# A two-block transformer kernel on one core: the first FFN opens with eight gate/up pairs instead of four

## The chip, the cores and the metric

The kernel runs on one NeuronCore of one Trainium2 chip. The metric is the device time of one execution in microseconds (us), from the first to the last instruction with what lies around them. A core has five engines that run their own instruction streams in order: TensorE (PE, matrix products into PSUM), VectorE (DVE), ScalarE (ACT), GpSimd (POOL) and SyncE (SP), which here issues almost all loads from device memory. PSUM, the memory that PE accumulates into, has eight banks of 512 float32 columns per partition.

## The reference

Two blocks work on one sequence of 256 tokens with 1024 features. The part that matters here is the very beginning: an RMS norm, a modulation whose scale and shift come from products of a small condition vector `c` with a large matrix `ada_w`, and a SwiGLU feed-forward network (FFN).

```
def rms_norm(x, g):
    xf = x.astype(jnp.float32)
    y = xf * lax.rsqrt(jnp.mean(xf * xf, axis=-1, keepdims=True) + EPS)
    return (y * g.astype(jnp.float32)).astype(x.dtype)

def swiglu(h, w_in, w_out):
    gu = h @ w_in
    g, u = jnp.split(gu, 2, axis=-1)
    return (jax.nn.silu(g) * u) @ w_out
...
        mods = jnp.split(c_silu @ ada_w[layer] + ada_b[layer], N_MOD, axis=-1)
        sh, sc, g = mods[0], mods[1], mods[2]
        h = modulate(rms_norm(x, norm_g[layer, 0]), sh, sc)
        x = x + MACARON_WEIGHT * (1.0 + g)[:, None, :] * swiglu(h, ffn_w_in[layer, 0], ffn_w_out[layer, 0])
```

There are four such FFNs (two layers, two each), a pooling mixer, an attention, and then a second block with a state-space branch and another attention. The hidden width of an FFN is 2816, which is 22 blocks of 128.

## The kernel before

Activations lie transposed: 128 features on the partitions, 256 tokens along the free axis, eight such feature blocks (`KB`). All numbers are float32. To multiply them exactly enough, every weight and every activation is split into a high part `hi` (rounded by ScalarE, `whi`, `hhi`, `shi`) and the rest `lo` (subtracted on VectorE, `wlo`, `hlo`, `slo`), and each product of blocks is three matmuls: `hi·hi`, `lo·hi`, `hi·lo` (`mm3`).

**Weights.** `Stream` loads weights as tiles of 128 x 1024 float32 (512 KB, eight blocks of 128 x 128) in the fixed order of use, into five raw buffers `wraw`. `split` rounds a tile on ScalarE (line 225, `whi`) and subtracts on VectorE (line 216, `wlo`), into five buffers each; the raw buffer is then free. One tile feeds 8 x 3 = 24 matmuls of 256 columns. The first FFN uses 66 tiles: 44 for the gate and up matrices, 22 for the output matrix. This text numbers them 0 to 65.

**Modulation.** Scale, shift and gate columns are products of the condition with rows of `ada_w`: one load of 512 KB into one of three buffers `graw`, one VectorE instruction over 128 x 1024 (line 377, called a product below). The first FFN's own scale and shift need 16 products, two for each feature block; 45 more, needed later, are spread over the tiles of the first FFN by `plan` and `tick`, so many per tile (`ffn_plan` gives the weights: none for the first tiles, 1.0 for the other gate/up tiles, 1.2 for the output tiles down to the last five).

**Opening of the first FFN.** There, the norm and the modulation of the eight feature blocks come one after the other, so the FFN goes by feature block first: for each `k`, `feed(k)` makes block `k` of the activation (`hraw` and `hlo` on VectorE, `hhi` on ScalarE) and splits one weight tile, and PE adds that block's contribution to four gate/up pairs, which are eight accumulators, one in each PSUM bank. After the eighth `k` the four pairs are finished by `act` (silu on ScalarE, a multiply `sf` on VectorE, and the split into `shi` and `slo`), and the other 18 pairs follow one at a time, two tiles each. In each `feed(k)` the products for the next feature blocks are placed on VectorE between the other work.

**Order.** Each engine executes in the order in which the program issued to it, and so does SP's queue of loads: a load that waits for its buffer holds up the loads behind it. Nothing is reordered at run time.

Of the kernel before, what the change touches and what calls it, by code (L numbers as in the profile page):

```python
# [12 lines left out]
AF = mybir.ActivationFunctionType  # L13
# [3 lines left out]
D = 1024  # L17
T = 256
KB = 8
# [4 lines left out]
RAWB, HLB = 5, 5  # L24
LAG = 1
HEAD_LAG = 1
GRAW = 3
# [3 lines left out]
W_OUT = (1.2, 1.6, 1.5, 1.6)  # L31
# [3 lines left out]
SLOTS = 135  # L35
# [6 lines left out]
def lead(l, f):  # L42
    return 4 if (l, f) == (0, 0) else 2

# [150 lines left out]
def ffn_plan(skip, w):  # L195
    return [0.0] * skip + [1.0] * (44 - skip) + [w] * 17


class Stream:
# [37 lines left out]
    def next(self, hold=False, late=None):  # L237
        if not hold:
            self.split(self.nh + self.ahead, late)
        r = self.split_t.pop(self.nh)  # L240
        self.nh += 1
        if self.nh >= 6 and self.ahead < HLB - 1:
            self.ahead += 1
            self.depth = RAWB
        return r


class Kernel:
# [15 lines left out]

# [1 line left out]
    def pool(self, name, bufs=1, **kw):  # L266
# [79 lines left out]

# [1 line left out]
    def mm3(self, out, hi, lo, b, ah, al, first, last):  # L348
        mm = self.nc.tensor.matmul
        mm(out, hi[:, b], ah, start=first, stop=False)  # L350
        mm(out, lo[:, b], ah, start=False, stop=False)  # L351
        mm(out, hi[:, b], al, start=False, stop=last)  # L352
# [92 lines left out]

# [1 line left out]
    def st_begin(self, n):  # L447
# [100 lines left out]

# [1 line left out]
    def ffn(self, hh, hl, gate_fn, n0, gap, pre, feed=None):  # L550
        nc = self.nc
        with self.tc.tile_pool(name="ffn", bufs=1) as fp:
# [3 lines left out]
            def act(i, pg, pu):  # L556
# [7 lines left out]
                if i == FB - 1:  # L564
                    self.after()
            tags = ("AB", "DD", "AB", "CC")
            pp = [[self.ps(t) for t in tags[i]] for i in range(n0)]
            b = 0
            for k in range(KB):
                if feed:  # L570
                    feed(k)
                for i in range(n0):
                    for x in range(2):
                        if b % 8 == 0:
                            hi, lo = self.next()
                        self.mm3(pp[i][x][:, :T], hi, lo, b % 8, hh[:, k], hl[:, k], k == 0, k == 7)
                        b += 1
            for i in range(n0):
                self.defer(act, i, *pp[i], lag=1 + HEAD_LAG * i)
            for i in range(n0, FB):  # L580
                pg, pu = [self.ps(t) for t in tags[(i - n0 // 4) % 3]]
# [35 lines left out]

# [1 line left out]
    def pool_mixer(self, hh, hl, gate_fn, pre):  # L619
# [34 lines left out]

# [1 line left out]
    def qk_stats(self, p, nch, th, ssq):  # L656
# [207 lines left out]

# [1 line left out]
    def setup(self):  # L866
# [22 lines left out]
    def phase1(self):  # L889
# [12 lines left out]
        with ExitStack() as p1:  # L902
# [15 lines left out]
            self.adab = load("adab", [128, NADA])  # L918
            self.ws.dma(1)
            onesr = const.tile([1, 128], F32, name="onesr")  # L920
# [41 lines left out]
            for i in range(2):  # L962
                nc.tensor.matmul(pc[i], onesr, crow[:, i * 512:(i + 1) * 512], start=True, stop=True)
            for kb in range(4):
                self.st_add(self.X[:, kb], nc.vector)
            for i in range(2):
                nc.scalar.activation(self.cb[:, i * 512:(i + 1) * 512], pc[i], AF.Silu)
            self.st_add(self.X[:, 4], nc.vector)
            head_gemv(0, 0)
            for kb in range(5, 8):  # L970
                self.st_add(self.X[:, kb])
            nc.scalar.activation(self.cc[:, 0], self.cc[:, 0], AF.Silu)
            head_dma(1, 2)
            head_gemv(0, 1)
            self.st_half(D)
            head_dma(2, 3)
            rb = self.st_finish()
            head_gemv(1, 0)
            weights = [0, 0, 3, 4, 5, 6, 7, 8, 9, 10, 11]
            splits = [1, 2, 3, 4, 5, 6, 7, 8]  # L980
# [11 lines left out]
            def feed(k):  # L992
                self.ws.ahead = self.ws.depth = 0
                c = slice(k, k + 1)
                a = slice(2 * k + 1, 2 * k + 2)
                V.scalar_tensor_tensor(g0[:, 0, c], self.modc[:, a], hg[:, 0, c], hg[:, 1, c],
                                       op0=OP.mult, op1=OP.add)
                a = slice(2 * k, 2 * k + 1)
                V.tensor_add(g0[:, 1, c], self.modc[:, a], self.adab[:, a])
                hr = self.mod_a(rbs, g0, h0[0], k)  # L1000
                if k + 1 < KB:
                    head_gemv(k + 1, 1)
                self.mod_b(hr, g0, h0[0], h0[1], k)
                self.ws.split(splits[k])
                if k + 2 < KB:
                    head_gemv(k + 2, 0)
                elif k + 1 == KB:
                    self.ws.ahead = self.ws.depth = 2
                if k + 3 < KB:
                    head_dma(k + 3, weights[k + 3])  # L1010
                else:
                    self.ws.dma(weights[k + 3])

# [7 lines left out]
            for l in range(2):  # L1021
# [7 lines left out]
                if l == 0:  # L1029
                    self.plan(self.gemvs(16, 64), ffn_plan(8, W_OUT[0]), ssm[0], SLOTS)  # L1030
                else:
                    self.plan(self.gemvs(base + 16, AT_A), ffn_plan(3, W_OUT[2]), ssm[3], SLOTS)
# [33 lines left out]

# [1 line left out]
    def vround(self, out, x, w):  # L1068
# [287 lines left out]

# [1 line left out]
    def hilo(self, hi, lo, src, w=None):  # L1358
# [500 lines left out]
```

## Time and profile before

| | |
|---|---|
| time, median of 3 runs | 1341.07 us (1338.28 to 1343.94) |
| span of the profiled execution | 1336.8 us |
| PE busy, share of the span | 96% |
| VectorE busy | 76% |
| ScalarE busy | 50% |
| mean rate of loads and stores over the span | 248 GB/s |

The span reaches from the first to the last instruction of one execution that was profiled; the page gives no other time for that execution. The runs without a profile are on the median 4.3 us above it, for what lies around the span. Busy shares are averages over stages that differ; what the change meets is read from the first 225 us.

### The profile page before, as it was taken

To read this page: it belongs to the slowest core of one execution; us is meant where nothing else is said; L and a number is where in the kernel's file an instruction comes from. 1 tells how busy PE (TensorE), PEld (TensorE's weight loads), DVE (VectorE), ACT (ScalarE), POOL (GpSimd) and SP (SyncE) were. 2 spreads that over 40 slices of the span, in tenths; PEclk is the share of its full clock that TensorE was granted. 3 is DMA by queue.
4 is the path that set the end of the run, shared out by engine and by line. 5 is a ranking of instruction groups with operands and counts; after the bars stand their busy time and mean duration, and the time that the engine had idled before them with its cause. 6 is when DMAs were issued, how large, how long until landed. Compare 5 with 4: busy or idle time off the path is not lost.

```text
span 1336.8 us, 26399 instructions
## 1 busy us (share of the span) xinstructions
PE 1276.9 (96%) x10378; PEld 1212.9 (91%) x10378; DVE 1011.1 (76%) x1759; ACT 668.6 (50%) x1162; POOL 159.0 (12%) x273
## 2 busy tenths in 40 slices
PE   5899999999999999999998999999999899999998
PEld 4899998899999779999987989999988888989996
DVE  6898887788999689989967678777754476437774
ACT  3454434555444555544436555444465755337542
POOL 1000001100002100010111101000100791110000
PEclk9999999999999999999999999999998999999999
DMA  8999998497899577999975368878765533796752
GB/s 293 332 330 342 331 337 300 145 325 251 266 318 341 199 268 264 309 301 308 343 266 182 120 216 258 266 249 279 264 222 174 146 114 106 161 242 204 271 186 79
DMA packets 122287, 331.21 MB, mean 248 GB/s; under 512 B 27633, under 2 KB 42865, under 8 KB 122098
## 3 DMA queue, kind: packets, MB, share of 16 engines
q1 hardware_dynamic: 122018, 328.73, 73.5%
q8 instruction: 81, 1.33, 0.4%
q0 software_dynamic: 144, 0.79, 0.2%
q14 instruction: 44, 0.36, 0.1%
HBM read 317.94 MB, written 10.49 MB: 246 GB/s over the span
## 4 chain that ended last, share of the span: by engine, by line
PE 55%; ACT 4%; DVE 3%; DMA 2%; issue 1%; POOL 1%; SPq 0%; DVEq 0%; ACTq 0%; POOLq 0%
PE psA L350 5%; PE psA L352 4%; PE psB L350 4%; PE psB L351 4%; PE psB L352 4%; PE psA L351 4%; PE psD L350 3%; PE psD L352 3%; PE psD L351 3%; PE psC L350 2%; PE psC L352 2%; PE psC L351 2%; PE psA L356 1%; PE psA L357 1%; PE psA L358 1%
## 5 line engine op out<-in xcount | busy, mean ns | idle before, releaser
L216 DVE TENSOR_TENSOR wlo<-wraw,whi 128x1024 fp32r<-128x1024 f32 x391 | 478.5, 1230 | 45.3 <-ACT whi L225 44.9
L225 ACT CAST whi<-wraw 128x1024 fp32r<-128x1024 f32 x391 | 403.1, 1047 | 115.9 <-ACT whi L225 40.1
L377 DVE SCALAR_TENSOR_TENSOR junk<-graw,cb 128x1024 bf16<-128x1024 f32 x166 | 204.5, 1232 | 27.7 <-DMA graw<-in_ada 23.8
L350 PE MATMUL psD<-hhi,whi 128*128 128x256 f32 x560 | 161.6, 289 | 0.0
L352 PE MATMUL psD<-hlo,whi 128*128 128x256 f32 x560 | 160.5, 287 | 0.0
L351 PE MATMUL psD<-hhi,wlo 128*128 128x256 f32 x560 | 160.4, 286 | 0.0
L350 PE MATMUL psA<-hhi,whi 128*128 128x256 f32 x480 | 139.2, 290 | 4.9 <-ACT whi L225 3.4
L351 PE MATMUL psA<-hhi,wlo 128*128 128x256 f32 x480 | 137.7, 287 | 6.0 <-DVE wlo L216 6.0
L350 PE MATMUL psB<-hhi,whi 128*128 128x256 f32 x488 | 139.3, 285 | 0.0
L351 PE MATMUL psB<-hhi,wlo 128*128 128x256 f32 x488 | 138.9, 285 | 0.0
L352 PE MATMUL psB<-hlo,whi 128*128 128x256 f32 x488 | 138.8, 284 | 0.0
L352 PE MATMUL psA<-hlo,whi 128*128 128x256 f32 x480 | 137.1, 286 | 0.0
L350 PEld LDWEIGHTS psD<-hhi,whi 128*128 128x128 f32 x560 | 109.3, 195 | 2.0 <-issue 1.4
L352 PEld LDWEIGHTS psD<-hlo,whi 128*128 128x128 f32 x560 | 109.3, 195 | 0.0
L351 PEld LDWEIGHTS psD<-hhi,wlo 128*128 128x128 f32 x560 | 109.3, 195 | 0.0
L350 PEld LDWEIGHTS psA<-hhi,whi 128*128 128x128 f32 x480 | 93.0, 194 | 8.5 <-ACT whi L225 4.7
L351 PEld LDWEIGHTS psA<-hhi,wlo 128*128 128x128 f32 x480 | 93.2, 194 | 7.4 <-DVE wlo L216 7.3
L350 PE MATMUL psA<-shi,whi 128*128 128x256 f32 x352 | 99.3, 282 | 0.0
L352 PE MATMUL psA<-slo,whi 128*128 128x256 f32 x352 | 98.7, 280 | 0.0
L350 PE MATMUL psB<-shi,whi 128*128 128x256 f32 x352 | 98.6, 280 | 0.0
L352 PE MATMUL psB<-slo,whi 128*128 128x256 f32 x352 | 98.6, 280 | 0.0
L351 PE MATMUL psB<-shi,wlo 128*128 128x256 f32 x352 | 98.2, 279 | 0.0
(452 smaller groups left out, 3198.1 us busy)
## 6 DMA issues: line engine op xcount, KB each, us to landing
graw<-in_ada SPq DMA_DIRECT2D x184, 512.0 KB
wraw<-in_win SPq DMA_DIRECT2D x176, 512.0 KB
wraw<-in_w SPq DMA_DIRECT2D x93, 512.0 KB
wraw<-in_wout SPq DMA_DIRECT2D x88, 512.0 KB
wraw<-in_wkv SPq DMA_DIRECT2D x16, 512.0 KB
Hd<-ct SPq DMA_DIRECT2D x16, 256.0 KB
Gd<-gsb SPq DMA_DIRECT2D x16, 256.0 KB
wraw<-in_wq SPq DMA_DIRECT2D x8, 512.0 KB
```

The lines of the kernel that those rows point to most:

```text
L216: self.nc.vector.tensor_sub(lo, raw, hi.bitcast(F32))
L225: self.nc.scalar.copy(hi, raw)
L350: mm(out, hi[:, b], ah, start=first, stop=False)
L351: mm(out, lo[:, b], ah, start=False, stop=False)
L352: mm(out, hi[:, b], al, start=False, stop=last)
L356: mm(out, ah, whi, start=first, stop=False)
L357: mm(out, ah, wlo, start=False, stop=False)
L358: mm(out, al, whi, start=False, stop=last)
L377: self.nc.vector.scalar_tensor_tensor(junk, self.gemv_tile(j), 1.0, self.cb, op0=OP.mult, op1=OP.mult, accum_out=self.modc[:, j:j + 1])
```

## The change

- The first FFN opens with eight pairs instead of four. A pair's gate and up sums now share one PSUM bank, 256 columns each, so that eight pairs fill the eight banks. `feed(k)` splits two weight tiles instead of one, and PE does 48 matmuls for each `k` instead of 24.
- In `feed(k)` the order on VectorE changes: the first tile's `wlo` comes before `hlo`, and the two products stand behind the two `wlo`.
- `act` for the pairs of the opening is called as soon as a pair's last matmul is issued, instead of one per later tile.
- The first norm's sums of squares are all added on VectorE (two additions were on GpSimd), and the products around it move.
- Two weight tiles instead of one are loaded before the first products' loads, and two instead of one for each `k` after that.
- The 45 spread products are now spread over fewer tiles, since 16 tiles instead of 8 belong to the opening.

```diff
-HEAD_LAG = 1
+LEAD = 8
...
 def lead(l, f):
-    return 4 if (l, f) == (0, 0) else 2
+    return LEAD if (l, f) == (0, 0) else 2
...
-        if self.nh >= 6 and self.ahead < HLB - 1:
+        if self.nh >= 2 * LEAD - 2 and self.ahead < HLB - 1:
...
-            tags = ("AB", "DD", "AB", "CC")
-            pp = [[self.ps(t) for t in tags[i]] for i in range(n0)]
+            tags = ("AB", "DD", "AB")
             b = 0
-            for k in range(KB):
-                if feed:
+            if feed:
+                pp = [self.ps(t) for t in "ABDDABCC"[:n0]]
+                for k in range(KB):
                     feed(k)
+                    for i in range(n0):
+                        for x in range(2):
+                            if b % 8 == 0:
+                                hi, lo = self.next()
+                            self.mm3(pp[i][:, x * T:(x + 1) * T], hi, lo, b % 8, hh[:, k], hl[:, k],
+                                     k == 0 and x == 0, k == 7, True)
+                            b += 1
+                        if k == KB - 1 and i:
+                            act(i - 1, pp[i - 1][:, :T], pp[i - 1][:, T:])
+                self.defer(act, n0 - 1, pp[n0 - 1][:, :T], pp[n0 - 1][:, T:])
...
-            self.ws.dma(1)
+            self.ws.dma(2)
...
-            for kb in range(4):
+            for kb in range(7):
                 self.st_add(self.X[:, kb], nc.vector)
-            for i in range(2):
-                nc.scalar.activation(self.cb[:, i * 512:(i + 1) * 512], pc[i], AF.Silu)
-            self.st_add(self.X[:, 4], nc.vector)
+                if kb == 3:
+                    for i in range(2):
+                        nc.scalar.activation(self.cb[:, i * 512:(i + 1) * 512], pc[i], AF.Silu)
+            self.st_half(D)
+            self.st_add(self.X[:, 7])
+            head_dma(1, 4)
             head_gemv(0, 0)
-            for kb in range(5, 8):
-                self.st_add(self.X[:, kb])
+            self.st_reduce()
             nc.scalar.activation(self.cc[:, 0], self.cc[:, 0], AF.Silu)
-            head_dma(1, 2)
             head_gemv(0, 1)
-            self.st_half(D)
-            head_dma(2, 3)
-            rb = self.st_finish()
-            head_gemv(1, 0)
+            head_dma(2, 6)
+            rb = self.st_spread()
...
                 hr = self.mod_a(rbs, g0, h0[0], k)
+                self.ws.split(2 * k + 1)
+                self.mod_b(hr, g0, h0[0], h0[1], k)
+                if k + 1 < KB:
+                    head_gemv(k + 1, 0)
+                self.ws.split(2 * k + 2)
                 if k + 1 < KB:
                     head_gemv(k + 1, 1)
-                self.mod_b(hr, g0, h0[0], h0[1], k)
-                self.ws.split(splits[k])
-                if k + 2 < KB:
-                    head_gemv(k + 2, 0)
-                elif k + 1 == KB:
+                else:
                     self.ws.ahead = self.ws.depth = 2
                 if k + 3 < KB:
-                    head_dma(k + 3, weights[k + 3])
+                    head_dma(k + 3, 2 * k + 8)
                 else:
-                    self.ws.dma(weights[k + 3])
+                    self.ws.dma(2 * k + 8)
...
-                    self.plan(self.gemvs(16, 64), ffn_plan(8, W_OUT[0]), ssm[0], SLOTS)
+                    self.plan(self.gemvs(16, 64), ffn_plan(2 * LEAD, W_OUT[0]), ssm[0], SLOTS)
```

The program's order on VectorE in one step of the opening, before the change: from one `hraw` to the next stand a product (`junk<-graw,cb`), `hlo`, one `wlo`, another product and two small instructions.

```order
L519 SCALAR_TENSOR_TENSOR hraw<-X,gain,rbs 128x256
L377 SCALAR_TENSOR_TENSOR junk,modc<-graw,cb 128x1024
L524 SCALAR_TENSOR_TENSOR hlo<-hraw,gain,hhi 128x256
L216 TENSOR_TENSOR wlo<-wraw,whi 128x1024
L377 SCALAR_TENSOR_TENSOR junk,modc<-graw,cb 128x1024
L996 SCALAR_TENSOR_TENSOR gain<-modc,gate 128x1
L999 TENSOR_TENSOR gain<-modc,adab 128x1
```

The same step after the change:

```order
L520 SCALAR_TENSOR_TENSOR hraw<-X,gain,rbs 128x256
L216 TENSOR_TENSOR wlo<-wraw,whi 128x1024
L525 SCALAR_TENSOR_TENSOR hlo<-hraw,gain,hhi 128x256
L378 SCALAR_TENSOR_TENSOR junk,modc<-graw,cb 128x1024
L216 TENSOR_TENSOR wlo<-wraw,whi 128x1024
L378 SCALAR_TENSOR_TENSOR junk,modc<-graw,cb 128x1024
L1007 SCALAR_TENSOR_TENSOR gain<-modc,gate 128x1
L1010 TENSOR_TENSOR gain<-modc,adab 128x1
```

There is one `wlo` more, and directly behind `hraw` now stands a `wlo`, where a product stood. On ScalarE, `hhi` of the step stands ahead of the step's roundings `whi`, both before and after; there are now two roundings.

The end of the opening on VectorE, after the change: the first two rows belong to the eighth `k`, then come the multiplies and subtractions of `act`, with the `wlo` of tiles 16 and 17 (`x2`) between those of the seventh pair (in `psC`).

```order
L525 SCALAR_TENSOR_TENSOR hlo<-hraw,gain,hhi 128x256
L216 TENSOR_TENSOR wlo<-wraw,whi 128x1024
L561 TENSOR_TENSOR sf<-sg,psA 128x256
...
L561 TENSOR_TENSOR sf<-sg,psC 128x256
L564 TENSOR_TENSOR slo<-sf,shi 128x256
L216 TENSOR_TENSOR wlo<-wraw,whi 128x1024 x2
L564 TENSOR_TENSOR slo<-sf,shi 128x256
L561 TENSOR_TENSOR sf<-sg,psC 128x256
L378 SCALAR_TENSOR_TENSOR junk,modc<-graw,cb 128x1024
L216 TENSOR_TENSOR wlo<-wraw,whi 128x1024 x2
```

Before, the `wlo` of the tile behind the opening followed the last tile of the opening at once (`x2`), ahead of any `sf`:

```order
L524 SCALAR_TENSOR_TENSOR hlo<-hraw,gain,hhi 128x256
L216 TENSOR_TENSOR wlo<-wraw,whi 128x1024 x2
L560 TENSOR_TENSOR sf<-sg,psB 128x256
L377 SCALAR_TENSOR_TENSOR junk,modc<-graw,cb 128x1024
L216 TENSOR_TENSOR wlo<-wraw,whi 128x1024 x2
```

So the first `wlo` behind the opening moved from ahead of the first pair's multiply to behind the seventh pair's.

## Rows read from the trace of the kernel before

**Rows 1.** The page: the span, and all engines' busy us (share of the span) x instructions.

```profile
span 1336.8 us, 26399 instructions
...
PE 1276.9 (96%) x10378; PEld 1212.9 (91%) x10378; DVE 1011.1 (76%) x1759; ACT 668.6 (50%) x1162; POOL 159.0 (12%) x273
```

**Rows 2.** All engines in order of time: start, duration, engine, line, instruction, [idle before].

```profile
8.35 0.43 DVE L470 TENSOR_TENSOR stacc<-stacc,stsq 128x256 f32<-128x256 f32 x1 [0.69 <-ACT stsq L465]
...
8.93 3.23 POOL L470 TENSOR_TENSOR stacc<-stacc,stsq 128x256 f32<-128x256 f32 x2 [7.99 <-DVE stacc L470]
...
14.12 0.16 DVE L503 TENSOR_REDUCE stm<-psC 128x2 f32<-128x4 f32 x1 [2.53 <-PE psC L501]
...
17.37 0.48 DVE L519 SCALAR_TENSOR_TENSOR hraw<-X,gain,rbs 128x256 f32<-128x256 f32 x1 [1.07 <-ACT rbs L982]
```

**Rows 3.** VectorE in order of time, one step of the opening.

```profile
21.90 0.48 DVE L519 SCALAR_TENSOR_TENSOR hraw<-X,gain,rbs 128x256 f32<-128x256 f32 x1
22.30 1.22 DVE L377 SCALAR_TENSOR_TENSOR junk<-graw,cb 128x1024 bf16<-128x1024 f32 x1
...
23.89 1.22 DVE L216 TENSOR_TENSOR wlo<-wraw,whi 128x1024 fp32r<-128x1024 f32 x1
25.04 1.22 DVE L377 SCALAR_TENSOR_TENSOR junk<-graw,cb 128x1024 bf16<-128x1024 f32 x1
...
26.43 0.48 DVE L519 SCALAR_TENSOR_TENSOR hraw<-X,gain,rbs 128x256 f32<-128x256 f32 x1
```

**Rows 4.** All engines in order of time, the opening's last step.

```profile
49.64 0.49 DVE L519 SCALAR_TENSOR_TENSOR hraw<-X,gain,rbs 128x256 f32<-128x256 f32 x1
...
50.57 1.98 ACT L225 CAST whi<-wraw 128x1024 fp32r<-128x1024 f32 x2
...
51.63 2.36 DVE L216 TENSOR_TENSOR wlo<-wraw,whi 128x1024 fp32r<-128x1024 f32 x2 [0.45 <-ACT whi L225]
```

**Rows 5.** PE in order of time, in the opening.

```profile
34.99 0.53 PE L351 MATMUL psA<-hhi,wlo 128*128 128x256 f32 x1 [1.63 <-DVE wlo L216]
...
35.54 0.42 PE L350 MATMUL psB<-hhi,whi 128*128 128x256 f32 x1
...
38.10 0.41 PE L350 MATMUL psB<-hhi,whi 128*128 128x256 f32 x1
```

**Rows 6.** PE in order of time: second matmuls of tiles 16, 17 and 60.

```profile
79.17 0.28 PE L351 MATMUL psD<-hhi,wlo 128*128 128x256 f32 x1
...
82.05 0.28 PE L351 MATMUL psD<-hhi,wlo 128*128 128x256 f32 x1
...
205.04 0.28 PE L351 MATMUL psB<-shi,wlo 128*128 128x256 f32 x1
```

**Rows 7.** VectorE in order of time: one `sf`, then `wlo` of tiles 22, 60 and 63.

```profile
65.76 0.42 DVE L560 TENSOR_TENSOR sf<-sg,psC 128x256 f32<-128x256 f32 x1 [0.23 <-ACT sg L558]
...
91.25 1.22 DVE L216 TENSOR_TENSOR wlo<-wraw,whi 128x1024 fp32r<-128x1024 f32 x1
...
200.84 1.22 DVE L216 TENSOR_TENSOR wlo<-wraw,whi 128x1024 fp32r<-128x1024 f32 x1
...
210.29 1.22 DVE L216 TENSOR_TENSOR wlo<-wraw,whi 128x1024 fp32r<-128x1024 f32 x1
```

**Rows 8.** Stretches: length, busy us (x count) by engine, PEclk, DMA share, GB/s.

```profile
100.00:150.00 50.00, 50.00 (x419) 50.00 (x419) 43.01 (x64) 24.18 (x36) 0.00 (x0) 1.00 0.96 347
150.00:200.00 50.00, 50.00 (x426) 50.00 (x425) 41.20 (x59) 20.59 (x26) 3.03 (x3) 1.00 0.93 326
200.00:222.00 22.00, 22.00 (x191) 21.87 (x192) 16.40 (x22) 7.15 (x9) 3.42 (x3) 1.00 0.97 354
```

**Rows 9.** Shorter stretches, same columns as Rows 8.

```profile
140.00:150.00 10.00, 10.00 (x86) 10.00 (x85) 9.16 (x15) 5.06 (x8) 0.00 (x0) 1.00 1.01 371
...
165.00:170.00 5.00, 5.00 (x45) 5.00 (x44) 3.57 (x5) 2.39 (x3) 0.00 (x0) 1.00 0.80 249
```

**Rows 10.** VectorE's waits from 56 to 222 us: total, times, longest.

```profile
DVE junk L377 <- DMA graw<-in_ada: 14.4, 11, 2.2
```

More of the change, by code (lines that the diff above doesn't have):

```diff
@@ L345, in flush, with mm3, mm @@
             f(*a)
-    def mm3(self, out, hi, lo, b, ah, al, first, last):
-        mm = self.nc.tensor.matmul
+    def mm3(self, out, hi, lo, b, ah, al, first, last, shared=False):
+        def mm(*a, **kw):
+            self.nc.tensor.matmul(*a, skip_group_check=shared, **kw)
         mm(out, hi[:, b], ah, start=first, stop=False)
@@ L565, in act @@
                     self.after()
-            tags = ("AB", "DD", "AB", "CC")
-            pp = [[self.ps(t) for t in tags[i]] for i in range(n0)]
+            tags = ("AB", "DD", "AB")
             b = 0
-            for k in range(KB):
-                if feed:
+            if feed:
+                pp = [self.ps(t) for t in "ABDDABCC"[:n0]]
+                for k in range(KB):
                     feed(k)
-                for i in range(n0):
[L573 to L579, printed above, removed]
+                    for i in range(n0):
[9 more added lines that the diff above has]
+            else:
+                pp = [[self.ps(t) for t in tags[i]] for i in range(n0)]
+                for k in range(KB):
+                    for i in range(n0):
+                        for x in range(2):
+                            if b % 8 == 0:
+                                hi, lo = self.next()
+                            self.mm3(pp[i][x][:, :T], hi, lo, b % 8, hh[:, k], hl[:, k], k == 0, k == 7)
+                            b += 1
+                for i in range(n0):
+                    self.defer(act, i, *pp[i], lag=1 + i)
             for i in range(n0, FB):
-                pg, pu = [self.ps(t) for t in tags[(i - n0 // 4) % 3]]
+                pg, pu = [self.ps(t) for t in tags[(i - (2 if feed else 0)) % 3]]
                 for half in range(2):
@@ L963, in phase1 @@
                 nc.tensor.matmul(pc[i], onesr, crow[:, i * 512:(i + 1) * 512], start=True, stop=True)
-            for kb in range(4):
+            for kb in range(7):
                 self.st_add(self.X[:, kb], nc.vector)
-            for i in range(2):
-                nc.scalar.activation(self.cb[:, i * 512:(i + 1) * 512], pc[i], AF.Silu)
-            self.st_add(self.X[:, 4], nc.vector)
+                if kb == 3:
[4 more added lines that the diff above has]
+            head_dma(1, 4)
             head_gemv(0, 0)
-            for kb in range(5, 8):
-                self.st_add(self.X[:, kb])
+            self.st_reduce()
             nc.scalar.activation(self.cc[:, 0], self.cc[:, 0], AF.Silu)
-            head_dma(1, 2)
             head_gemv(0, 1)
-            self.st_half(D)
-            head_dma(2, 3)
-            rb = self.st_finish()
-            head_gemv(1, 0)
-            weights = [0, 0, 3, 4, 5, 6, 7, 8, 9, 10, 11]
-            splits = [1, 2, 3, 4, 5, 6, 7, 8]
+            head_dma(2, 6)
+            rb = self.st_spread()
             rbs = self.tmp.tile([128, T], F32, name="rbs", bufs=1)
@@ L1000, in feed @@
                 hr = self.mod_a(rbs, g0, h0[0], k)
+                self.ws.split(2 * k + 1)
[3 more added lines that the diff above has]
+                self.ws.split(2 * k + 2)
                 if k + 1 < KB:
                     head_gemv(k + 1, 1)
-                self.mod_b(hr, g0, h0[0], h0[1], k)
-                self.ws.split(splits[k])
-                if k + 2 < KB:
-                    head_gemv(k + 2, 0)
-                elif k + 1 == KB:
+                else:
                     self.ws.ahead = self.ws.depth = 2
                 if k + 3 < KB:
-                    head_dma(k + 3, weights[k + 3])
+                    head_dma(k + 3, 2 * k + 8)
                 else:
-                    self.ws.dma(weights[k + 3])
+                    self.ws.dma(2 * k + 8)
             def half_gate(l, m):
```

## The prediction

> **What bounds the kernel now.** I read the page first. PE is busy for 96% of the span [rows 1], so a change pays only where PE waits or where it starts later than it must. I then followed the first 225 us in order of time, engine by engine. The reader is to see three things there. First, up to 17.37 us PE has nothing to do, because the norm's sum is late: two additions on GpSimd take 3.23 us and end at 12.16, the reduction follows at 14.12, and the first `hraw` at 17.37 [rows 2]. Second, in the opening VectorE sets the pace: a step lasts from one `hraw` to the next, 26.43 - 21.90 = 4.53 us [rows 3], while a tile's 24 matmuls take 82.05 - 79.17 = 2.88 us on PE [rows 6], 0.12 each. Third, from tile 8 to the end of the FFN PE runs without a gap (50 us busy of 50 in a stretch), and what lies close behind it is the loads: 326 to 354 GB/s at a share of 0.93 to 0.97 [rows 8], with VectorE waiting 14.4 us for `graw` [rows 10].
>
> **The start.** The two additions go to VectorE, at 0.43 us each. Three in a row from 8.35 end at about 9.6 instead of GpSimd's 12.16. The rest of the chain is as long as before (12.16 to 14.12, 14.12 to 17.37 [rows 2]), so the first `hraw` comes at about 14.85, **2.5 us earlier**. The two products that now stand between its links, 1.22 us each [rows 3], fit into the 1.96 and 3.25 us in which VectorE would wait anyway. The second weight tile, loaded ahead of the products, arrives long before its step asks for it.
>
> **The step.** Before, the step's 4.53 us were VectorE's work without a pause. The change adds a `wlo`, 25.04 - 23.89 = 1.15 us [rows 3]. It also puts a `wlo` directly behind `hraw`, and that `wlo` needs a rounding that stands behind `hhi` on ScalarE, which needs `hraw`. The opening's last step before, where no product filled the gap, shows how long this chain is: `hraw` at 49.64, `wlo` at 51.63, 1.99 us, the last part of it idle [rows 4]. With a product in its place the next instruction came 22.30 - 21.90 = 0.40 us behind `hraw` [rows 3]. So a step now takes 4.53 + 1.15 + (1.99 - 0.40) = **7.27 us**. PE needs 48 x 0.12 = 5.8 us of it and idles some 1.5; four loads at 347 GB/s, 1.51 us each [rows 8], need 6.0 us and are hidden.
>
> The last `hraw` is at 14.85 + 7 x 7.27 = 65.7. Its `wlo` begins 1.99 later and lasts 1.22, `hlo` now comes behind it (0.4), and the remaining 46 matmuls take 5.5: the opening ends at 74.9. The clock is a side term: after a wait of 1.63 us PE ran 12 matmuls in 38.10 - 35.54 = 2.56 us, 0.213 each, the 1.2 GHz level instead of 2.4 [rows 5]. If this happens in a step, its idle 1.5 us cover it; in the last step it would cost 0 to 1.5 us. I take 0.
>
> **The handover.** The `wlo` of tile 16 now stands behind the seventh pair's multiply. That pair's last matmul is 6 x 0.12 = 0.7 us before the end, at 74.2; silu, multiply and one subtraction follow, each about as long as the multiply's 0.42 [rows 7], then the `wlo` of 1.22. Tile 16's second matmul can start at **76.65**. Before, it started at 79.17 [rows 6]. So the larger opening brings nothing beyond the start: PE is 2.5 us ahead. If PE never waited again, tile 60 would come at 76.65 + (205.04 - 79.17) = 202.5, and the whole gain would be 2.5 us.
>
> **The debt.** In the old program five of the 45 spread products were done by tile 16, now none. They are spread over fewer tiles, and by tile 60 the program has placed 58 products both before and after. From `wlo` 22 to `wlo` 60 VectorE must now work off 38 tiles and 38 products, 76 loads; before it was 38 and 32, 70 loads. At the handover some seven loads lie ready in the buffers; with them VectorE reaches the end of `wlo` 22 at about 90.0 (six `wlo`, four products at 1.15 each, five small ones at 0.4). PE asks for tile 22 at 76.65 + 6 x 2.88 = 93.9. Up to tile 60 PE needs 125.87 - 6 x 2.88 = 108.6 us. So 3.9 + 108.6 = 112.5 us are there for 76 loads, **1.48 us for a load of 512 KB**; at any slower pace PE waits 76p - 112.5 us. At the end of the stretch there is then no lead left, and the three `wlo` to tile 63 take 210.29 - 200.84 = 9.45 us [rows 7] against PE's three tiles at 2.83 = 8.5: **1.0 us** more.
>
> The pace p is the disputed size. Before, the same tiles took 202.06 - 92.47 = 109.6 us for 70 loads, 1.566 each [rows 7]. In part PE held it back then. The stretches give 1.481 us (354 GB/s), 1.511 (347) and 1.608 (326) [rows 8]. Now the buffers never fill, so I expect it better than 1.566, but not as good as the best 22 us: I take 1.54, between 1.511 and 1.566. PE then waits 76 x 1.54 - 112.5 = 4.5 us.
>
> **The sum**: -2.5 + 4.5 + 1.0 = +3.0 us. On the profiled execution, 1336.8 us become 1339.8; on the median, which lies 4.3 us above that span, 1341.07 becomes **1344.1 us**. Behind the first FFN nothing is changed, and the loads pause after it, so that the debt isn't carried on. The bounds: no wait at all gives -2.5, p = 1.608 gives 9.7 - 2.5 + 1.0 = +8.2. I count 0.5%, 6.7 us, as what a measurement of this kernel can tell from no change: below 1334.4 is faster, above 1347.8 slower.
>
> **Rivals.**
> 1. *The queue keeps up.* If loads that are always waiting run at the best rate seen, 354 GB/s over 22 us or 371 over 10 us at a full share [rows 8, 9], p is 1.48 or less and PE doesn't wait: -2.5 us, **1338.6**. For it speaks that the slower stretches had shares below 1; against it that SP's loads wait in order for buffers, which stays so. The Trainium skill, "DMA: Bandwidth & Descriptors" (Specifications), gives a core's share of device memory as about 358 GB/s; by that rule a load takes an estimated 1.46 us and this rival would hold. The 50 us stretches of this trace stay below that figure, the shorter ones reach it. Chance 0.22.
> 2. *Slower.* Only three `graw` buffers feed the products, and the output tiles now carry 18 products between tiles 44 and 60 instead of 15. A product that waits holds the `wlo` behind it, and this holds SP's next load; the stretch from 165 to 170 us ran at 249 GB/s and a share of 0.80 for this [rows 9]. If such holes are as frequent all along as from 150 to 200 (326 GB/s), the time is +8.2 us, **1349.3**. It decides from p = 1.59 on, where the sum passes 6.7 us. Chance 0.14.
> 3. *The change does all that it can.* Were the rounding early, so that VectorE's step had no hole, the step would be bound by four loads, 6.0 us, and the opening would end 7 x 1.27 = 8.9 us earlier, with the loads running on. The debt would shrink by as much: -2.5 - 8.9 = -11.4 at best, less 1 to 2 for the loads, about **1331**. Against it stands the order on ScalarE, where `hhi` of the step is ahead of its roundings [rows 4]. Chance 0.04.
>
> **How the numbers follow.** The forecast (PE waits some us in the FFN's later tiles, p between 1.49 and 1.59, 1340 to 1347.8) has a chance of 0.60, the rivals 0.22, 0.14 and 0.04. Faster is the third and a trace of the first: 0.05. Slower is the second: 0.14. The rest, 0.81, is within 0.5%. The range from 1337 to 1349 takes in the first rival and most of the second; the spread of the three runs, 2.8 us to either side, is in it.
>
> **What would show it.** In the profile after, `hraw` first at about 14.9, then every 7.3 us, each time with an idle VectorE of about 1.5 us ahead of a `wlo` that waits for `whi`; tile 16's second matmul near 76.7; fewer loads outstanding than before around 65 to 77 us; then PE waiting for `wlo`, mostly in the output tiles, 2 to 7 us in total; the FFN's end 1 to 5 us later than before. Steps near 6 us, or no PE wait between 77 and 210, would prove the sum wrong; so would any difference behind 225 us.

## The result, and the profile after

The changed kernel is **slower**: 1352.0 us median (1348.74 to 1355.34, 4 runs) against 1340.81 us of the kernel before on the same chip (4 runs), a ratio of 1.0074 with a 95% interval of 1.0054 to 1.0093. The forecast of 1344.1 us was too low, and the time lies above its range. The profiled execution took 1352.14 us, its span is 1350.4 (before 1336.8 [rows 1]). The page of the changed kernel, the span and the first line of busy times:

```profile
span 1350.4 us, 26395 instructions
...
PE 1281.2 (95%) x10378; PEld 1214.7 (90%) x10378; DVE 1013.4 (75%) x1761; ACT 667.2 (49%) x1162; POOL 160.3 (12%) x271
```

PE is busy for 4.3 us longer for the same number of matmuls, so part of the loss is slower matmuls, and the rest, 1350.4 - 1336.8 - 4.3 = 9.3 us of the span, waiting. I followed the first 237 us in order of time, as before.

**The opening went as forecast.** VectorE in the changed kernel in order of time, one step (start, duration, engine, line, instruction, [idle before <- what ended it]); `wlo` is L216, `hraw` now L520:

```profile
14.56 0.48 DVE L520 SCALAR_TENSOR_TENSOR hraw<-X,gain,rbs 128x256 f32<-128x256 f32 x1 [1.06 <-ACT rbs L993]
16.56 1.22 DVE L216 TENSOR_TENSOR wlo<-wraw,whi 128x1024 fp32r<-128x1024 f32 x1 [1.51 <-ACT whi L225]
17.70 0.48 DVE L525 SCALAR_TENSOR_TENSOR hlo<-hraw,gain,hhi 128x256 fp32r<-128x256 f32 x1
...
21.89 0.48 DVE L520 SCALAR_TENSOR_TENSOR hraw<-X,gain,rbs 128x256 f32<-128x256 f32 x1
...
65.91 0.48 DVE L520 SCALAR_TENSOR_TENSOR hraw<-X,gain,rbs 128x256 f32<-128x256 f32 x1
```

`hraw` comes 2.8 us earlier than before [rows 2], and the step lasts 21.89 - 14.56 = 7.33 us, with the hole of 1.51 us ahead of the `wlo` that waits for its rounding.

**The handover did not.** VectorE and then ScalarE in the changed kernel, from the first pair's `act` to the `wlo` of tiles 16 and 17; `sg` is silu, `sf` the multiply, `shi` its rounding:

```profile
70.78 0.42 DVE L561 TENSOR_TENSOR sf<-sg,psA 128x256 f32<-128x256 f32 x1
71.96 0.42 DVE L561 TENSOR_TENSOR sf<-sg,psB 128x256 f32<-128x256 f32 x1 [0.76 <-ACT sg L559]
...
76.20 0.42 DVE L561 TENSOR_TENSOR sf<-sg,psD 128x256 f32<-128x256 f32 x1 [1.75 <-ACT sg L559]
...
79.73 0.42 DVE L561 TENSOR_TENSOR sf<-sg,psC 128x256 f32<-128x256 f32 x1 [0.42 <-ACT sg L559]
80.07 0.42 DVE L564 TENSOR_TENSOR slo<-sf,shi 128x256 fp32r<-128x256 f32 x1
80.40 2.35 DVE L216 TENSOR_TENSOR wlo<-wraw,whi 128x1024 fp32r<-128x1024 f32 x2
```

```profile
70.37 0.39 ACT L559 ACTIVATE sg<-psA 128x256 f32<-128x256 f32 x1 [1.54 <-PE psA L350]
71.24 0.41 ACT L563 CAST shi<-sf 128x256 fp32r<-128x256 f32 x1 [0.49 <-DVE sf L561]
71.55 0.38 ACT L559 ACTIVATE sg<-psB 128x256 f32<-128x256 f32 x1
...
73.90 1.99 ACT L225 CAST whi<-wraw 128x1024 fp32r<-128x1024 f32 x2
75.80 0.37 ACT L559 ACTIVATE sg<-psD 128x256 f32<-128x256 f32 x1
...
79.32 0.38 ACT L559 ACTIVATE sg<-psC 128x256 f32<-128x256 f32 x1
```

The two engines wait for each other in turn: `shi` of one pair waits for `sf`, the next pair's `sg` stands behind `shi`, the next `sf` waits for `sg`. That is 71.55 - 70.37 = 1.18 us a pair, while PE finishes a pair every 6 x 0.12 = 0.7 us. Seven pairs, with the rounding of tiles 16 and 17 between (1.9 us), hold the `wlo` of tile 16 until 80.40. What PE did (all three matmuls of `mm3` are L350 now; second matmuls of tiles 16, 17 and 18, then 51 and 52, then 59 and 60; the last row on VectorE is the FFN's end):

```profile
81.68 0.58 PE L350 MATMUL psA<-hhi,wlo 128*128 128x256 f32 x1 [6.20 <-DVE wlo L216]
...
86.96 0.41 PE L350 MATMUL psA<-hhi,wlo 128*128 128x256 f32 x1
...
90.02 0.28 PE L350 MATMUL psD<-hhi,wlo 128*128 128x256 f32 x1
...
186.88 0.39 PE L350 MATMUL psA<-shi,wlo 128*128 128x256 f32 x1 [1.98 <-DVE wlo L216]
190.67 0.39 PE L350 MATMUL psA<-shi,wlo 128*128 128x256 f32 x1 [0.72 <-DVE wlo L216]
...
214.89 0.58 PE L350 MATMUL psB<-shi,wlo 128*128 128x256 f32 x1 [3.17 <-DVE wlo L216]
...
220.18 0.41 PE L350 MATMUL psB<-shi,wlo 128*128 128x256 f32 x1
...
237.22 0.48 DVE L546 SCALAR_TENSOR_TENSOR X<-psB,gate,X 128x256 f32<-128x256 f32 x1 [5.07 <-PE psB L350]
```

PE waits 6.20 us at the handover, and then needs 86.96 - 81.68 = 5.28 us for a tile that takes 2.88 [rows 6], 0.22 a matmul: the 1.2 GHz level, with a granted clock of 0.50 from 82 to 87 us. The same happens behind the wait of 3.17 us (220.18 - 214.89 = 5.29, a granted clock of 0.50 from 215 to 220). Stretches of the changed kernel (length, busy us of PE, PEld, VectorE, ScalarE, GpSimd, granted clock, DMA share, GB/s):

```profile
60.00:85.00 25.00, 17.03 (x118) 15.82 (x118) 18.11 (x33) 14.22 (x26) 0.00 (x0) 0.91 0.55 198
85.00:100.00 15.00, 15.00 (x119) 15.00 (x118) 12.34 (x18) 6.63 (x9) 0.00 (x0) 0.92 0.94 345
100.00:150.00 50.00, 50.00 (x419) 50.00 (x418) 43.85 (x67) 22.46 (x34) 0.00 (x0) 1.00 0.95 337
150.00:200.00 50.00, 47.16 (x394) 46.54 (x393) 40.63 (x60) 18.30 (x26) 1.21 (x2) 1.00 0.93 328
200.00:220.00 20.00, 16.69 (x119) 16.08 (x118) 16.93 (x22) 7.28 (x9) 3.96 (x3) 0.84 0.91 329
```

At the handover the loads thin out as well, to 198 GB/s and a share of 0.55: the chain holds the `wlo` that free `wraw`, and from 65 to 85 us SP's loads of `wraw` wait for nothing else, in one case 10.6 us. Where PE waits later, the queue runs at 328 GB/s and a share of 0.93, not at its best [rows 8].

**Where the time went.** The FFN ends at 237.22, before at 222.08 (the same row of the kernel before): +15.1, where +3.0 was forecast. Of the 12.1 between, the handover is 81.68 - 76.65 = 5.0; the slow clock behind two waits 2 x 2.4 = 4.8; from tile 44 to tile 59 PE needs 49.99 us instead of 42.41, 7.6 more where 4.5 was forecast, 3.1; tile 17 takes 0.2 more; the tail lasts as long as before instead of 1.0 longer. Behind the FFN the profiled spans differ by 1113.2 - 1114.7 = -1.5 us. The medians differ by 11.2, the spans by 13.6: the span of before lies 4.0 us below its median, that of the changed kernel 1.6. What lies around a span is 1.7 to 1.9 us in every run that lists both, so some 2.5 of the 4.3 us that the table of before puts down to it were a quick execution; the forecast adds a difference to the median, so it does not change by this.

### The profile page after: what moved, and what is told of

Same layout as the page of the kernel before. It is cut to its first block, busy times and chain, and to the rows that moved or that the text cites. A ratio compares the mean times of both kernels' runs of the same rounds, so it can differ in the third digit from the quotient of the medians.

```text
span 1350.4 us, 26395 instructions
## 1 busy us (share of the span) xinstructions
PE 1281.2 (95%) x10378; PEld 1214.7 (90%) x10378; DVE 1013.4 (75%) x1761; ACT 667.2 (49%) x1162; POOL 160.3 (12%) x271
## 4 chain that ended last, share of the span: by engine, by line
PE 52%; ACT 4%; DVE 4%; DMA 3%; issue 1%; SPq 1%; POOL 1%; DVEq 0%; ACTq 0%; POOLq 0%
PE psA L350 13%; PE psB L350 13%; PE psD L350 9%; PE psC L350 5%; DMA Hs<-Hd 1%; PE psA L357 1%; DVE wlo L216 1%; PE psA L358 1%; PE psA L359 1%; PE psB L357 1%; PE psB L359 1%; PE psB L358 1%; ACT qjunk L675 1%; ACT whi L225 1%; PE psD L1764 1%
## 5 line engine op out<-in xcount | busy, mean ns | idle before, releaser
L216 DVE TENSOR_TENSOR wlo<-wraw,whi 128x1024 fp32r<-128x1024 f32 x391 | 479.6, 1232 | 55.6 <-ACT whi L225 55.1
L350 PE MATMUL psD<-hhi,whi 128*128 128x256 f32 x560 | 160.6, 287 | 0.4 <-ACT hhi L521 0.4
L350 PE MATMUL psD<-hlo,whi 128*128 128x256 f32 x560 | 159.5, 285 | 0.0
L350 PE MATMUL psD<-hhi,wlo 128*128 128x256 f32 x560 | 159.3, 284 | 0.0
L350 PE MATMUL psA<-hhi,wlo 128*128 128x256 f32 x472 | 135.8, 288 | 12.0 <-DVE wlo L216 12.0
L350 PE MATMUL psA<-hhi,whi 128*128 128x256 f32 x472 | 136.9, 290 | 4.0 <-ACT whi L225 2.5
L350 PE MATMUL psB<-hhi,whi 128*128 128x256 f32 x480 | 137.2, 286 | 0.0
L350 PE MATMUL psB<-hhi,wlo 128*128 128x256 f32 x480 | 137.1, 286 | 0.0
L350 PE MATMUL psB<-hlo,whi 128*128 128x256 f32 x480 | 137.0, 285 | 0.0
L350 PE MATMUL psA<-hlo,whi 128*128 128x256 f32 x472 | 135.8, 288 | 0.1
L350 PEld LDWEIGHTS psD<-hhi,whi 128*128 128x128 f32 x560 | 108.5, 194 | 2.1 <-issue 1.4
L350 PEld LDWEIGHTS psD<-hlo,whi 128*128 128x128 f32 x560 | 108.4, 193 | 0.2 <-DVE hlo L525 0.2
L350 PEld LDWEIGHTS psD<-hhi,wlo 128*128 128x128 f32 x560 | 108.4, 194 | 0.0
L350 PEld LDWEIGHTS psA<-hhi,wlo 128*128 128x128 f32 x472 | 91.8, 194 | 13.8 <-DVE wlo L216 13.7
L350 PE MATMUL psB<-shi,wlo 128*128 128x256 f32 x352 | 99.8, 284 | 3.4 <-DVE wlo L216 3.2
L350 PE MATMUL psA<-shi,wlo 128*128 128x256 f32 x352 | 98.6, 280 | 2.7 <-DVE wlo L216 2.7
L350 PE MATMUL psB<-shi,whi 128*128 128x256 f32 x352 | 99.5, 283 | 0.0
L350 PE MATMUL psB<-slo,whi 128*128 128x256 f32 x352 | 99.5, 283 | 0.0
L350 PE MATMUL psA<-shi,whi 128*128 128x256 f32 x352 | 99.2, 282 | 0.0
L350 PE MATMUL psA<-slo,whi 128*128 128x256 f32 x352 | 98.4, 280 | 0.0
```

The costliest lines, as they stand in the source:

```text
L216: self.nc.vector.tensor_sub(lo, raw, hi.bitcast(F32))
L350: self.nc.tensor.matmul(*a, skip_group_check=shared, **kw)
```

## The experiments

All start from the changed kernel, except e7. Ratios are to the kernel before on the same chip; the end is that of the first FFN in the profiled execution, the pace the mean time of a load between `wlo` 22 and `wlo` 60. The profiles are one execution each. Where PE hardly waits, the pace is about what PE asks for: 108.6 us for these 76 loads, 1.43 each, or 1.55 for the 70 of before and e7.

| run | what | median us | ratio, 95% interval | FFN end | pace |
|---|---|---|---|---|---|
| before | | 1340.81 | 1 | 222.08 | 1.566 |
| changed | | 1352.0 | 1.0074 (1.0054 to 1.0093) | 237.22 | 1.587 |
| e1 | `wlo` 16, 17 early | 1349.75 | 1.0077 (1.0063 to 1.0090) | 232.96 | 1.546 |
| e5 | acts deferred | 1343.84 | 1.0037 (1.0021 to 1.0053) | 230.23 | 1.618 |
| e2 | no hole | 1337.19 | 0.9975 (0.9962 to 0.9989) | 224.67 | 1.561 |
| e3 | e1 + e2 | 1339.63 | 1.0007 (0.9994 to 1.0020) | 223.08 | 1.556 |
| e6 | e2 + e5 | 1335.66 | 0.9977 (0.9959 to 0.9995) | 215.57 | 1.573 |
| e4 | half the bytes of 45 loads | 1343.02 | 1.0019 (1.0003 to 1.0035) | 226.03 | 1.453 |
| e10 | control for e9 | 1349.94 | 1.0060 (1.0039 to 1.0081) | 235.45 | 1.557 |
| e9 | four `graw` buffers | 1344.97 | 1.0028 (1.0013 to 1.0043) | 226.72 | 1.481 |
| e11 | products spread evenly | 1342.75 | 1.0007 (0.9994 to 1.0020) | 226.51 | 1.459 |
| e7 | before, only the norm on VectorE | 1338.72 | 0.9991 (0.9974 to 1.0008) | 221.83 | 1.546 |
| e8 | e6 + e11 | 1331.5 | 0.9941 (0.9919 to 0.9963) | 214.49 | 1.532 |
| e12 | e8 + four `graw` buffers | 1331.24 | 0.9919 (0.9906 to 0.9932) | 213.15 | 1.444 |

**The handover.** The first question was whether the place of one `wlo` costs the time, or the chain of acts as a whole. e1 issues the `wlo` of tiles 16 and 17 ahead of the fourth pair's act:

```diff
                             if b % 8 == 0:
                                 hi, lo = self.next()
+                                if k == KB - 1 and i:
+                                    self.los()
```

> The changed kernel with the subtractions (wlo) of tiles 16 and 17 issued ahead of the fourth pair's act instead of behind the seventh pair's. Theory A (the chain of act on ScalarE and VectorE, about 1.18 us a pair, holds wlo 16 to 81.6 us and so costs PE a wait of 6.2 us and a slow stretch behind it): tile 16's second matmul near 76.5 us instead of 81.7, no slow stretch, the first FFN ends 6 to 8 us earlier than the changed kernel's (237.2 us), ratio to the kernel before near 1.003. Rival B (the loads' pace alone sets the FFN's end, so time saved at the handover is given back as later waits): tile 16 as early, but the FFN's end moves by less than 2 us, ratio near 1.008.

PE's waits in e1:

```profile
76.29 0.39 PE L350 MATMUL psA<-hhi,wlo 128*128 128x256 f32 x1 [0.79 <-DVE wlo L216]
...
86.64 0.58 PE L350 MATMUL psD<-hhi,wlo 128*128 128x256 f32 x1 [3.58 <-DVE wlo L216]
```

Tile 16 comes 5.4 us earlier, and tile 18 waits 3.58 us instead, again with the slow clock behind: its roundings and `wlo` still stand behind the chain. The FFN ends 4.3 us earlier in the profile, between what the two theories expected, and the ratio to before shows nothing of it. So that one `wlo` alone is not the cause. e5 takes the chain apart, each act behind a later tile, as the kernel before did:

```diff
-                        if k == KB - 1 and i:
-                            act(i - 1, pp[i - 1][:, :T], pp[i - 1][:, T:])
-                self.defer(act, n0 - 1, pp[n0 - 1][:, :T], pp[n0 - 1][:, T:])
+                for i in range(n0):
+                    self.defer(act, i, pp[i][:, :T], pp[i][:, T:], lag=max(1, i))
```

> The changed kernel with act for the opening's eight pairs spread again, one per later tile (the first two behind the opening's last tile), instead of all at once. The first experiment showed that wlo 16 alone doesn't free PE, since the chain of act holds tile 18 instead. Theory A2 (the whole chain of eight acts, about 1.18 us each on two engines that wait for each other, is the cost of the handover): no PE wait above 1 us between 72 and 100 us, tile 17's second matmul near 79 us instead of 87.0, and since loads start again earlier too, the FFN ends 6 to 9 us earlier than the changed kernel's 237.2, ratio near 1.003. Rival B (loads' pace takes it all): FFN end above 234, ratio 1.007 or more.

Tile 16's second matmul is at 75.73 and tile 17's at 78.97, and neither waits. In their place PE waits 2.9 us, in three pieces, for banks that a deferred act has not read yet:

```profile
83.27 0.38 PE L350 MATMUL psD<-hhi,whi 128*128 128x256 f32 x1 [1.02 <-DVE sf L561]
...
90.22 0.39 PE L350 MATMUL psB<-hhi,whi 128*128 128x256 f32 x1 [0.93 <-DVE sf L561]
...
96.83 0.39 PE L350 MATMUL psA<-hhi,whi 128*128 128x256 f32 x1 [0.96 <-ACT sg L559]
```

The end is 7.0 us earlier, and the median agrees (1.0037 against 1.0074). The chain of seven acts is the handover's cost.

**The step's hole.** e2 moves the step's first product, and `hlo`, ahead of the first `wlo`, as the kernel before had a product there:

```diff
                 hr = self.mod_a(rbs, g0, h0[0], k)
-                self.ws.split(2 * k + 1)
-                self.mod_b(hr, g0, h0[0], h0[1], k)
                 if k + 1 < KB:
                     head_gemv(k + 1, 0)
+                self.mod_b(hr, g0, h0[0], h0[1], k)
+                self.ws.split(2 * k + 1)
                 self.ws.split(2 * k + 2)
```

> The changed kernel with each step's first product and hlo put back between hraw and the two wlo, so that the hole in VectorE's step is filled. By the rows of before a step is then 4.53 + 1.15 = 5.7 us of VectorE or 6.0 us of loads instead of 7.33, and the opening's last step begins 9 to 11 us earlier. Theory A (PE's waits and VectorE's hole are the cost, loads follow): FFN's end 8 to 10 us earlier than the changed kernel's, ratio near 1.001. Rival B (loads' pace sets the end): most of it is given back, FFN's end less than 4 us earlier, ratio near 1.006.

The step falls from 7.33 to 5.80 us, and PE waits in the same way at the handover, only earlier:

```profile
72.56 0.58 PE L350 MATMUL psA<-hhi,wlo 128*128 128x256 f32 x1 [6.20 <-DVE wlo L216]
```

The end comes 12.5 us earlier, more than expected. At the handover it is 81.68 - 72.56 = 9.1: the step is now about VectorE's own work (4.53 + 1.15) and PE's (5.8), and behind 18 us PE does not wait in the opening. The other 3.4 us come behind the handover, where PE's waits in the output tiles and the slow clock behind them are shorter. So the third rival had priced the hole about right (8.9 us), though its bound, four loads in 6.0 us, does not bind at 5.80, and the cure does not need an earlier rounding. e3 joins e1 and e2, e6 joins e2 and e5.

> Both edits, wlo 16 and 17 early and the hole filled. Theory A: the two add up, 14 to 18 us off the changed kernel's FFN end of 237.2 us, ratio near 0.997. Rival B: the loads' pace (1.55 to 1.59 us per 512 KB) binds from the opening on, the FFN ends no earlier than about 228 us, ratio 1.000 to 1.004.

> Act spread and the hole in the step filled. The opening ends near 66 us, no PE wait there. Theory A2: FFN end at 214 to 218 us, 5 to 8 us earlier than before the change (222.1), ratio 0.994 to 0.996. Rival B (loads at 1.55 us each bind): FFN end 220 to 224 as with the hole alone, ratio 0.997 to 1.001.

e6 gains what the two gain apart (237.22 - 12.5 - 7.0 = 217.7, measured 215.57), while its ratio stays above the 0.994 to 0.996 that were expected. In e3, too, the stall moves to tile 18 (76.61, a wait of 3.58). Its median is 2.4 us above that of e2 with an end 1.6 us earlier; this stays open, and the last section shows what moves behind the FFN.

**The loads behind the handover.** Here the question was whether the bytes, the buffers, or the places of the products make PE wait late. In e4 each of the 45 spread products loads half of its rows' columns and uses that half twice, so the modulation's values change (the edit of the product is left out here):

```diff
-            self.nc.sync.dma_start(t, self.h["ada"][i])
+            if 16 <= i < 61:
+                self.nc.sync.dma_start(t[:, :512], self.h["ada"][i][:, :512])
+            else:
+                self.nc.sync.dma_start(t, self.h["ada"][i])
...
```

> The changed kernel with the 45 spread products of the first FFN loading only the first half of each row tile (256 KB instead of 512 KB) and using that half twice, so that VectorE's work stays and only bytes go; this changes the modulation values that these products give. Rival B (loads' pace): PE's waits behind tile 17 vanish, FFN's end near 227 us instead of 237, ratio near 1.000. Theory A alone (the handover is the only cost): less than 2 us change.

After the handover PE never waits, at only 274 GB/s in the stretch from 100 to 150. Loads matter, then; but it doesn't tell bytes from waiting for them. e9 leaves the bytes and gives the products a fourth buffer (`sg` gives up one of two, in later stages too, and a constant most of its columns); e10 does the same without the buffer:

```diff
-GRAW = 3
+GRAW = 4
...
-                sg = self.tmp.tile([128, T], F32, name="sg", bufs=2)
+                sg = self.tmp.tile([128, T], F32, name="sg", bufs=1)
```

> The changed kernel with four graw buffers instead of three (to make room, sg has one buffer instead of two, and a constant of 64 columns has 4). It tells whether the products' buffers or the bytes set the pace of the loads behind the handover. If the buffers do (the second rival of the prediction): VectorE's waits for graw, 18.9 us in 24 pieces in the changed kernel, fall below 10 us, the pace from wlo 22 to wlo 60 falls from 1.587 to about 1.52 us per load, PE's waits at 186.88, 190.67 and 214.89 (5.9 us, and 2.4 us of slow clock behind the last) mostly go, and the FFN ends 5 to 8 us earlier, at 229 to 232. If the rate of the transfers does: a pace of 1.57 or more, an end of the FFN within 2 us of 237.2, a time of 1350 to 1354 us. The wait of 6.2 us for tile 16's wlo stays in both.

> The control for the run with four graw buffers: the changed kernel with one buffer for sg and the shorter constant, and three graw buffers. Silu of one pair now waits until the multiply of the pair before has read sg; in the opening's end this chain was already one pair behind the other, 1.18 us for each. Expected: 0 to 2 us later than the changed kernel, 1350 to 1355 us, the FFN's end at 237 to 239. If it is more, the four-buffer run has to be compared with this one.

The same stretches of e9, with the columns as above:

```profile
100.00:150.00 50.00, 50.00 (x419) 50.00 (x418) 43.73 (x66) 24.07 (x35) 0.00 (x0) 1.00 0.97 357
150.00:200.00 50.00, 50.00 (x424) 50.00 (x423) 46.93 (x68) 22.14 (x28) 3.42 (x3) 1.00 0.96 359
200.00:220.00 20.00, 20.00 (x172) 20.00 (x171) 17.27 (x23) 7.68 (x9) 2.15 (x2) 1.00 0.98 364
```

And VectorE's waits for `graw` from 82 to 227 us (total, times, longest), in the changed kernel and in e9:

```profile
DVE junk L378 <- DMA graw<-in_ada: 18.9, 24, 2.0
```

```profile
DVE junk L378 <- DMA graw<-in_ada: 3.9, 4, 1.6
```

With the same bytes the queue moves 359 GB/s instead of 328, PE has no wait behind the handover, and the FFN ends 8.7 us before the control's, further than expected. The device's rate is not what held the loads. The control behaved like the changed kernel (late waits up to 3.25 us, an end 1.8 us earlier). How the buffers hold them shows in SP's queue of the changed kernel, beside VectorE's rows of the same time:

```profile
181.80 0.33 SPq L211 DMA_DIRECT2D wraw<-in_wout  x1
182.18 1.34 SPq L364 DMA_DIRECT2D graw<-in_ada  x2
```

```profile
179.40 1.23 DVE L378 SCALAR_TENSOR_TENSOR junk<-graw,cb 128x1024 bf16<-128x1024 f32 x1 [1.58 <-DMA graw<-in_ada]
...
180.55 1.22 DVE L216 TENSOR_TENSOR wlo<-wraw,whi 128x1024 fp32r<-128x1024 f32 x1
181.93 1.23 DVE L378 SCALAR_TENSOR_TENSOR junk<-graw,cb 128x1024 bf16<-128x1024 f32 x1 [0.16 <-DMA graw<-in_ada]
...
184.45 1.23 DVE L378 SCALAR_TENSOR_TENSOR junk<-graw,cb 128x1024 bf16<-128x1024 f32 x1 [1.28 <-DMA graw<-in_ada]
...
185.60 1.22 DVE L216 TENSOR_TENSOR wlo<-wraw,whi 128x1024 fp32r<-128x1024 f32 x1
188.25 1.22 DVE L378 SCALAR_TENSOR_TENSOR junk<-graw,cb 128x1024 bf16<-128x1024 f32 x1 [1.43 <-DMA graw<-in_ada]
```

The product at 179.40 is done with its buffer at 180.63, but the load that refills it goes out only at 182.18: ahead of it in the queue stands a load of `wraw`, and that goes out at 181.80, when the `wlo` that frees its buffer ends. With three buffers in turn this load of `graw` is for the third product behind, the one at 188.25, which waits 1.43 us for it, and the next `wlo` stands behind that product. Once VectorE has no lead, each load waits for a VectorE that waits for a load. e11 keeps three buffers and moves products:

```diff
-W_OUT = (1.2, 1.6, 1.5, 1.6)
+W_OUT = (1.0, 1.6, 1.5, 1.6)
```

> The changed kernel with the 45 spread products placed evenly over the gate/up and the output tiles (weight 1.0 for an output tile instead of 1.2), so that a few more of them stand in the gate/up tiles. Same loads, same bytes. If PE's late waits come from where the debt falls due (18 products between tiles 44 and 60): the wait of 3.2 us at 214.89 falls below 2 us and the slow clock behind it (2.4 us) does not come, the FFN ends 2 to 5 us earlier, at 232 to 235; the waits near 186 grow. If only the sum of the bytes counts: the end within 1 us of 237.2 and the slow clock stays. The wait of 6.2 us for tile 16's wlo stays in both.

Only two products move from the tiles behind 44 to those ahead. More came of it than expected (an end of 232 to 235): no wait of PE behind the handover, an end of 226.51, 372 GB/s from 100 to 150 us. VectorE still waits 12.6 us for `graw`, in 19 pieces, but its `wlo` always end 1.5 us or more ahead of PE at the tiles from 56 to 60, where the changed kernel had 0.06 at tiles 56 and 58. The traces show where two products are worth so much. In the changed kernel VectorE does one product or none ahead of each `wlo` behind the handover, but two ahead of those of tiles 51 and 59 (the rows at 181.93 and 184.45 are those of tile 51), and these are the tiles for which PE waits 1.98 and 3.17 us. In e1, e2, e3, e5, e6 and e10, with the same places, the longest late wait is at tile 59, too (1.16 to 3.39 us). In e11 no tile has two. In e4, with half the bytes, and in e9, with a fourth buffer, the same two tiles keep their two products and PE waits at neither.

**The start alone.** e7 is the kernel before with its two GpSimd additions on VectorE:

```diff
             for kb in range(5, 8):
-                self.st_add(self.X[:, kb])
+                self.st_add(self.X[:, kb], nc.vector)
```

> The kernel before with one part of the change alone: the norm's last two additions on VectorE. First hraw 1 to 2.5 us earlier than 17.37 us (the first product then stands behind them); PE was not held by loads in the kernel before, so the FFN's end moves by as much, 220 to 221 us, ratio 0.998 to 0.999. Rival: given back at the first wait for a product's load, no change of the FFN's end.

The first `hraw` is at 15.52, 1.85 us earlier, and the last at 49.45 instead of 49.64 [rows 4]: two steps of the opening lengthen, VectorE's waits for `graw` from 15 to 56 us grow from 1.5 to 3.2 us, the end moves by 0.25 us, and the time is that of before. So the rival of the expectation came about: an earlier start is worth nothing where the next stage waits for its loads.

**All together.** e8 and e12 put together what helped.

> As the kernel with act spread and the hole filled, and the 45 spread products evenly over the tiles (weight 1.0 instead of 1.2 on the output tiles), which is 15 to 16 products between tiles 44 and 60 instead of 18. If where the products stand matters (three graw buffers), PE's waits of the output tiles, up to 3 us each, shrink and the FFN ends 2 to 4 us earlier; if only the total of loads matters, less than 1 us.

The end of e8 is only 1.1 us earlier than that of e6, against 2 to 4 expected, while its median is 4.2 us below that of e6 on the same chip; the larger part of this is not explained by the end, and stays open.

> The fastest version so far (a product ahead of the first wlo in each step, the eight acts deferred, the spread products even), with four graw buffers and one sg buffer. In that version PE still waited 1.0, 1.3, 0.4 and 0.8 us, and the pace was 1.520 us per load. If the graw buffers limited it: the last three waits go, the FFN ends at 211 to 213 instead of 214.5, about 1329 us. If the transfers limit it: within 1 us of 214.5, 1331 to 1334 us, a ratio to the kernel before of 0.993 to 0.996.

e12 from 100 us on:

```profile
100.00:150.00 50.00, 50.00 (x419) 50.00 (x418) 47.43 (x75) 24.65 (x35) 0.00 (x0) 1.00 1.00 385
150.00:200.00 50.00, 50.00 (x427) 50.00 (x426) 46.45 (x61) 21.73 (x26) 5.87 (x5) 1.00 0.97 369
```

Eight pairs in the opening are then faster than four: 1331.24 us, a ratio of 0.9919 (0.9906 to 0.9932) to the kernel before. The fourth buffer brings the FFN's end 1.3 us forward here; PE's waits of 0.36 and 0.81 us in the output tiles are gone with it. The end lies between the two expectations, the median in that of the transfers, and the intervals of e8 and e12 overlap, so the run does not tell the two apart. The kernel before was not run with the even spread or a fourth buffer; its PE waits for nothing from 56 us to the end of the FFN, so little is to be expected of them there, but no run shows it.

## Why the prediction was wrong

- *The start*, -2.5 us: right (14.56 for 14.85; 0.5 us of it is that the first additions began at 5.69 instead of 6.17 in this execution). Alone the start was worth nothing (e7).
- *The step*, 7.27 us with an idle of 1.5: right (7.33 and 1.51).
- *The handover*, tile 16 at 76.65: **this step failed.** It took the seventh pair's own act, behind that pair's last matmul at 74.2, and no queue ahead of it. The seven acts are one chain over two engines at 1.18 us a pair, slower than PE's 0.7, and the two roundings stand in it: 5.0 us, and 2.4 us for the slow clock behind a wait of 6.2. e1 and e5 show that it is the chain. The clock was a side term, taken as 0 to 1.5 us in the last step and not asked for in any wait that the sum itself forecast.
- *The debt*, 76 loads at 1.54 us: its form was right, PE waits in the output tiles, but p was mis-sized: 1.587 us a load, by which 76p - 112.5 is 8.1 us, and 7.6 were lost up to tile 59 instead of 4.5, with 2.4 us more from the clock. The pace was read from stretches as if it were the device's. e9 and e11 show that it follows from three buffers in one queue in order and from where the products stand: the two long waits, 1.98 and 3.17 us, are those of the two tiles with two products ahead of their `wlo`. The second rival had this mechanism, in the output tiles and from p = 1.59 on. As it stood nearly there, with the handover's loss on top, the time passed that rival's 1349.3.
- *The first rival* (the queue keeps up) did not come about in the changed kernel, but the queue can do it: 357 to 385 GB/s over 50 us in e9 and e12. The Trainium skill, "DMA: Bandwidth & Descriptors" (Specifications), gives about 358 GB/s as a core's share; e12's 385 over 50 us lies above that figure, so here the measurement decides. Of the shorter stretches that the prediction set beside it only the one of 10 us (371) reached it; that of 22 us stayed at 354.
- *The tail*, +1.0: it was 0, the same 17.04 us from tile 60's second matmul to the end in both kernels. The slow clock at tile 59 had given VectorE a lead of 2.85 us at tile 60, where the prediction counted on none.

## What to carry to other kernels

When work is called "as soon as its input is ready", count the chain that it forms on the engines it runs through, per item and over all items, and what stands behind it there; compare the time per item with that of the producer. A wait of TensorE can have a second price behind it, where the clock falls. A pace read from a queue in order may be that of its buffers and not of the device; a run with one more buffer tells. And a change that costs as it stands may gain once such a place is mended: here the same eight pairs went from 0.7% slower to 0.8% faster.

## What the runs showed of the hardware that was not expected

In the changed kernel the slow clock came behind the waits of 6.20 and 3.17 us, each time for about one tile and 2.4 us, and not behind those of 1.98 and 0.72; behind e1's 3.58 a tile cost 1.5 us more (86.64 to 91.02), behind the same wait in e3 2.4 (76.61 to 81.90). The length of the wait alone does not decide it: in e6 the slow clock came behind a wait of 1.92 us (the next tile took 4.39 us, at a granted clock of 0.60 from 86.7 to 91), and the price behind the same wait of 6.2 us at the handover was from 1.4 us (e4) to 2.4.

The rest of the program, of which e9, e10 and e12 changed the buffers of `sg` and the other experiments nothing, took from 1111.5 to 1119.8 us in the profiles. PE's busy time there for the same number of matmuls went from 1069.7 us (e9) to 1077.3 (e8), and the granted clock was 0.99 in four of the five quickest and 0.98 in the others. One stretch in e9 (1112.7 us behind the FFN), then in e11 (1119.5):

```profile
720.00:780.00 60.00, 52.53 (x398) 46.40 (x397) 42.30 (x104) 35.26 (x90) 10.21 (x9) 0.97 0.40 130
```

```profile
720.00:780.00 60.00, 54.51 (x399) 47.88 (x397) 42.74 (x104) 34.94 (x90) 9.30 (x9) 0.94 0.40 133
```

Nearly the same matmuls ran there at a mean clock of 0.97 in the one execution and of 0.94 in the other. This goes some way to explain why runs of one kernel spread by several us, and why an end of the FFN that moves by 1 or 2 us is not always seen in a median; e2, the quickest behind the FFN at a clock of 0.98, does not fit it.
